# Modulation rows of a two-layer hybrid block moved and paired, last down tiles split once, values projected token-major

## The chip, the cores and the metric

The kernel runs on one core of a Trainium2 chip. The metric is the device time of one execution in microseconds (us); the number that stands for a kernel is the median of its runs. The engines that matter are TensorE (PE in the profile; its weight loads are PEld), VectorE (DVE), ScalarE (ACT), GpSimd (POOL) and SyncE (SP), which issues nearly all transfers.

## What is computed

A generator block of two layers over 512 latent tokens and 256 context tokens, 1024 channels. Cut to what matters here:

```python
for l in range(DEPTH):                       # 2 layers
    need_ctx = l < DEPTH - 1                 # context tokens only matter in layer 0
    sh1, sc1, g1, sh2, sc2, g2 = jnp.split(sc @ w_ada[l] + b_ada[l], 6, axis=-1)   # modulation
    ...
    h = rmsnorm(x, norm1_g[l]) * (1.0 + sc1) + sh1
    ...
    y, yc = hybrid_mixer(h, hc, w_in[l], ...)
    x = x + g1 * y
    h = rmsnorm(x, norm2_g[l]) * (1.0 + sc2) + sh2
    x = x + g2 * swiglu(h, w_ffn_gate[l], w_ffn_up[l], w_ffn_down[l])
    ...
# hybrid_mixer
aq, ak, av, bq, bzf, bzb, bi, bg, cu, cv, gt = split_proj(h @ w_in)
a = window_attention(...); b = hgrn_readout(hgrn2_bidir(... v=bi ...), bg, ...); c = chunk_mlp(cu, cv, ...)
# merge
g = sigmoid(gt.reshape(..., 3, D))
m = g[0] * (a @ w_br[0]) + g[1] * (b @ w_br[1]) + g[2] * (c @ w_br[2])
y = m @ w_o
```

In layer 0 all of it is done for the 512 latent and the 256 context tokens, 768 columns; in layer 1 the context matters only for keys, values and the HGRN states. `bi` are the values of the HGRN recurrence (4 heads of 128), `cv` the half of the gMLP that is mixed over tokens (4 tiles of 128 channels).

## The kernel before, in words

Activations lie channel-major: 128 channels on the partitions, tokens along the free axis. A projection (`dense`) takes one tile of 128 output channels: the weight tile (k x 128 x 128, k = 8 for 1024 inputs) is loaded raw by SP into one of three buffers (`wr`), ScalarE rounds it to its high half (`wh`), VectorE subtracts to get the low half (`wl`, line 296), and PE runs three matmuls per k (high by high, high by low, low by high) into a PSUM tile of 1024 columns (`pd`, two buffers). 768 tokens are a 512- and a 256-column matmul. The high and low halves of a weight tile have a buffer pair of their own kind, and the framework that orders the instructions puts the split of a tile about one tile ahead of its matmuls on each engine.

Work that PE needs little of runs as "chains", generators that `spent` steps on by an amount of PE time credited by `dense` (HGRN scans, norms, attention). SBUF beside the weights is cut in pages; a page is held as two halves (`single`) or whole (`pair`).

**Modulation.** A unit is 512 of the 6144 outputs of `w_ada`, 8 rows of 128 x 512. Layer 0's first four units are made at the start by matmul. The others go row by row on VectorE: `ada_accum` multiplies a row by the conditioning and adds it to `acc` (line 531; two `acc` where the context needs it too, one otherwise); after 8 rows a transpose and a reduce (lines 506, 507). `fill` takes one row from a queue through one buffer (`aw`), and asks for the next row's load once the row is used. `fill_unit` takes a whole unit, two rows per load, through `wr`. Before, 24 rows run as `fill_unit` between HGRN heads of layer 0, 48 in layer 0's merges (two `fill` for each of 24 tiles), others in layer 0's FFN, and 32 in layer 1's merges (two for each tile of the second and third branch).

**Order of a layer**: projections of the 4 HGRN heads; keys; attention with gMLP and HGRN gates between; merges (three branches, eight tiles `m` each: a gate tile of `w_in` with k = 8, a branch tile with k = 4, line 1300 on); output; FFN in pieces (gate and up tiles, then 8 down tiles for each piece). In layer 0's last FFN pieces the gate and up tiles are made by a scheme with seven products in place of eight (`seven`). The last piece's down tiles run once for each of two blocks of tokens (layer 0: 512 and 256, layer 1: 256 and 256), so that the norm that follows can begin on the first block; each block loads and splits its tiles anew. `norm_begin`, `start_settle` and `norm_end` make the next layer's input (`nt`, `hl`, lines 721 and 731).

**HGRN values and gMLP v.** Both are needed with tokens on the partitions. Before, they are projected channel-major, copied by ScalarE to `vf` or `cvs`, transposed on PE by 128 x 128 against an identity, and copied back (`V`, `cvt`).

## Time and profile before

| | us |
|---|---|
| median of 3 runs | 2484.31 (2484.30 to 2485.63) |
| profiled execution | 2482.72 |
| its span on the core | 2480.9 |
| projections of layer 0 | 47.5 to 533 |
| merges of layer 0 | 533 to 843 |
| output of layer 0 | 843 to 921.4 |
| FFN of layer 0, with its last down tiles | 921.4 to 1466 |
| projections of layer 1 | 1466 to 1836 |
| merges of layer 1 | 1836 to 2054 |
| output of layer 1 | 2054 to 2104 |
| FFN of layer 1, then the final norm | 2104 to 2480.9 |

The page is one execution taken by the hardware profiler. Names are those of the program: `pd<-hh,wl` is a matmul into a projection's PSUM tile from an activation and a weight half, and a line number is that of the kernel before. "Idle before" is the time that an engine stood still just before an instruction, with what ended it.

### The profile page before, as it was taken

The page shows a single profiled execution, that of the slowest core. Times are in us where ns is not written, and L with a number is a line of the kernel's source. Part 1 is how long each engine was busy: PE and PEld are TensorE (multiplying, and loading weights), DVE is VectorE, ACT ScalarE, POOL GpSimd, SP SyncE. Part 2 cuts the span into 40 slices and gives each one's busy share as a digit, 9 for nine tenths or more (in the row PEclk, how much of TensorE's full clock was granted, in tenths as well). Part 3 has the DMA queues.
Part 4 walks back from the last instruction along what each step waited for, and adds up shares of the span by engine and source line. Part 5 has one row for each costly group of instructions (what it writes and reads, how often), then busy time and mean ns, then how long its engine had stood idle before and what let it go on. Part 6 is the DMA issues. An engine that isn't in the chain of part 4 may idle for free. (4 is left out here: it accounts for less than half of the span.)

```text
span 2480.9 us, 34528 instructions
## 1 busy us (share of the span) xinstructions
PE 2397.0 (97%) x13606; PEld 2083.7 (84%) x13606; DVE 1555.1 (63%) x2644; ACT 900.3 (36%) x1508; POOL 308.9 (12%) x215
## 2 busy tenths in 40 slices
...
GB/s 295 70 77 81 48 43 35 39 64 112 142 133 73 78 118 43 115 111 110 95 127 111 107 144 52 43 43 52 60 44 152 124 151 168 79 106 100 91 103 130
DMA packets 370673, 240.02 MB, mean 97 GB/s; under 512 B 9744, under 2 KB 341968, under 8 KB 370512
## 3 DMA queue, kind: packets, MB, share of 16 engines
...
q8 instruction: 107, 1.75, 0.3%
...
q14 instruction: 54, 0.44, 0.1%
...
## 5 line engine op out<-in xcount | busy, mean ns | idle before, releaser
L295 ACT ACTIVATE wh<-wr 128x1024 fp32r<-128x1024 f32 (+4 forms) x344 | 308.0, 895 | 853.1 <-PE pd L313 727.2
L313 PE MATMUL pd<-hh,wl 128*128 128x512 f32 (+1 forms) x1504 | 451.9, 356 | 21.5 <-DVE wl L296 21.4
L296 DVE TENSOR_TENSOR wl<-wr,wh 128x1024 fp32r<-128x1024 f32 (+4 forms) x344 | 354.9, 1032 | 186.8 <-ACT wh L295 184.1
L313 PE MATMUL pd<-hh,wh 128*128 128x512 f32 (+1 forms) x1504 | 459.9, 362 | 0.7 <-ACT wh L295 0.6
L313 PE MATMUL pd<-hl,wh 128*128 128x512 f32 (+1 forms) x1504 | 446.7, 354 | 0.0
L313 PEld LDWEIGHTS pd<-hh,wl 128*128 128x128 f32 x1504 | 249.0, 190 | 65.7 <-DVE wl L296 28.9
L531 DVE SCALAR_TENSOR_TENSOR acc<-wra,sc,acc 128x512 f32<-128x512 f32 x224 | 169.6, 778 | 186.7 <-DMA wra<-in_w_ada 175.6
L313 PEld LDWEIGHTS pd<-hl,wh 128*128 128x128 f32 x1504 | 248.2, 190 | 34.4
L313 PEld LDWEIGHTS pd<-hh,wh 128*128 128x128 f32 x1504 | 249.7, 191 | 31.4 <-ACT wh L295 1.0
L313 PE MATMUL pd<-fh,wl 128*128 128x512 f32 (+1 forms) x496 | 175.3, 370 | 0.3 <-DVE wl L296 0.3
L313 PE MATMUL pd<-fl,wh 128*128 128x512 f32 (+1 forms) x496 | 175.7, 370 | 0.0
L313 PE MATMUL pd<-fh,wh 128*128 128x512 f32 (+1 forms) x496 | 174.4, 369 | 0.6 <-ACT silu L1370 0.6
L313 PE MATMUL pd<-guh,wh 128*128 128x512 f32 (+1 forms) x576 | 172.6, 341 | 1.8 <-ACT guh L760 0.9
L313 PE MATMUL pd<-guh,wl 128*128 128x512 f32 (+1 forms) x576 | 172.5, 340 | 1.8 <-DVE wl L296 1.8
L313 PE MATMUL pd<-gul,wh 128*128 128x512 f32 (+1 forms) x576 | 172.9, 340 | 0.1
L808 DVE SCALAR_TENSOR_TENSOR X<-pd,mod,X 128x256 f32<-128x256 f32 (+1 forms) x160 | 84.1, 560 | 85.3 <-PE pd L313 84.9
L313 PEld LDWEIGHTS pd<-guh,wh 128*128 128x128 f32 x576 | 98.3, 188 | 15.4 <-ACT guh L760 1.2
L313 PEld LDWEIGHTS pd<-guh,wl 128*128 128x128 f32 x576 | 98.6, 189 | 15.1 <-DVE wl L296 2.6
L313 PEld LDWEIGHTS pd<-gul,wh 128*128 128x128 f32 x576 | 98.7, 189 | 13.4 <-DVE gul L761 0.9
L313 PEld LDWEIGHTS pd<-fh,wl 128*128 128x128 f32 x496 | 90.1, 188 | 17.4 <-DVE wl L296 1.2
L313 PEld LDWEIGHTS pd<-fh,wh 128*128 128x128 f32 x496 | 89.5, 188 | 16.8 <-ACT silu L1370 0.8
L313 PEld LDWEIGHTS pd<-fl,wh 128*128 128x128 f32 x496 | 90.0, 188 | 15.5
...
## 6 DMA issues: line engine op xcount, KB each, us to landing
wr<-in_w_in SPq DMA_DIRECT2D x116, 512.0 KB, 3.9
wra<-in_w_ada SPq DMA_DIRECT2D x136, 256.0 KB, 2.8
wr<-in_w_ffn_gate SPq DMA_DIRECT2D x44, 512.0 KB, 3.9
wr<-in_w_ffn_up SPq DMA_DIRECT2D x44, 512.0 KB, 3.9
wr<-in_w_out SPq DMA_DIRECT2D x32, 512.0 KB, 3.7
wr<-in_w_branch SPq DMA_DIRECT2D x48, 256.0 KB, 3.0
wr<-in_w_ffn_down SPq DMA_DIRECT2D x48, 256.0 KB, 2.8
...
```

What stands on the lines that cost most here:

```text
L295: nc.scalar.activation(out=h, in_=r, func=AF.Copy)
L296: nc.vector.tensor_tensor(out=o, in0=r, in1=h.bitcast(F32), op=ALU.subtract)
L313: nc.tensor.matmul(ps[:, b0:b1], lhsT=w[:, k, :], rhs=x[:, b0:b1], start=b not in first, stop=(k == kt - 1 and i == 2), skip_group_check=True)
L531: nc.vector.scalar_tensor_tensor(out=acc[:, 0:512], in0=w, scalar=sc, in1=acc[:, 0:512], op0=ALU.mult, op1=ALU.add)
L808: self.nc.vector.scalar_tensor_tensor(out=self.X[m][:, c0:c1], in0=ps[:, c0:c1], scalar=gcol(b, m), in1=self.X[m][:, c0:c1], op0=ALU.mult, ...
```

## The change

1. `dense_tokens`: HGRN values for two heads at a time (with the even head), and gMLP v for two tiles at a time. The activations are the stationary operand (128 tokens), a weight block of 128 x 256 moves, the result has tokens on the partitions and is copied straight to `V` or `cvt`. The weights come as two loads of four k each. 768 tokens are six chunks, four in one `pd` and two in the other. The transposes and the copies through `vf` and `cvs` go.
2. Modulation: `fill_pairs` takes two rows per load of 512 KB through `wr`. Layer 0's merges take one pair per tile in place of two single rows. Layer 1's merges take none; of their 32 rows, 16 (units 8 and 9) are queued behind layer 0's merges, with one more `fill` in each group of seven products, and 16 (units 10 and 11) run as two pairs behind each of the first four gate and up tiles of layer 1's FFN.
3. `keep_w`: in the last FFN piece the first block splits each down tile into a page pair (`wk`), and the second block uses it again.
4. At the head of each branch of the merges, chains are stepped on until six page pairs are free.

The loads that SP issues go from 582 to 534, and PE's matmuls grow by 300 (192 in the HGRN values, 192 in gMLP v, 4 for the modulation, less 88 transposes).

VectorE in layer 0's merges, second branch, before: `acc` with two rows (each twice, for latent and context), `gt` the gate's product with the branch, `wl` of 512 columns a branch tile's split and of 1024 a gate tile's.

```order
L1323 SCALAR_TENSOR_TENSOR gt_6130<-gt_6130,pd_6138 128x768
L296 TENSOR_TENSOR wl_6233<-wr_6230,wh_6232 128x512
L531 SCALAR_TENSOR_TENSOR acc_6426<-wra_6665,sc,acc_6426 128x512
L531 SCALAR_TENSOR_TENSOR acc_6427<-wra_6665,sc,acc_6427 128x512
L531 SCALAR_TENSOR_TENSOR acc_6426<-wra_6724,sc,acc_6426 128x512
L531 SCALAR_TENSOR_TENSOR acc_6427<-wra_6724,sc,acc_6427 128x512
L506 STREAM_TRANSPOSE tr_6763<-acc_6426 128x512
L506 STREAM_TRANSPOSE tr_6766<-acc_6427 128x512
L507 TENSOR_REDUCE parts_5615<-tr_6763 128x16
L507 TENSOR_REDUCE parts_5615<-tr_6766 128x16
L296 TENSOR_TENSOR wl_6270<-wr_6267,wh_6269 128x1024
L1323 SCALAR_TENSOR_TENSOR gt_6228<-gt_6228,pd_6236 128x768
```

The same place now (the number in `wra_` is the load):

```order
L303 TENSOR_TENSOR wl_6562<-wr_6559,wh_6561 128x1024
L1357 SCALAR_TENSOR_TENSOR gt_6516<-gt_6516,pd_6524 128x768
L303 TENSOR_TENSOR wl_6619<-wr_6616,wh_6618 128x512
L565 SCALAR_TENSOR_TENSOR acc_6553<-wra_6745,sc,acc_6553 128x512
L565 SCALAR_TENSOR_TENSOR acc_6554<-wra_6745,sc,acc_6554 128x512
L565 SCALAR_TENSOR_TENSOR acc_6553<-wra_6745,sc,acc_6553 128x512
L565 SCALAR_TENSOR_TENSOR acc_6554<-wra_6745,sc,acc_6554 128x512
L303 TENSOR_TENSOR wl_6658<-wr_6655,wh_6657 128x1024
L1357 SCALAR_TENSOR_TENSOR gt_6614<-gt_6614,pd_6622 128x768
L303 TENSOR_TENSOR wl_6715<-wr_6712,wh_6714 128x512
```

Before, the rows of two loads stand between the two splits; now the four `acc` between them come from one load, with the same count of instructions per tile.

VectorE at layer 0's last down tiles, second block, before: `X` 128x256 is the residual of a down tile of that block, `wl` 128x512 a down tile's split, `nt` and `hl` the norm for layer 1.

```order
L808 SCALAR_TENSOR_TENSOR X_6771<-pd_12829,mod_141,X_6771 128x256
L680 TENSOR_TENSOR sqa_12800<-sqa_12800,sq_12820 128x512
L296 TENSOR_TENSOR wl_12875<-wr_12872,wh_12874 128x512
L649 TENSOR_SCALAR ms_12858<-st_12853 128x4
L808 SCALAR_TENSOR_TENSOR X_6771<-pd_12849,mod_141,X_6771 128x256
L296 TENSOR_TENSOR wl_12900<-wr_12897,wh_12899 128x512
L721 SCALAR_TENSOR_TENSOR nt_12916<-X_6771,A_12611,rsb_12885 128x512
L808 SCALAR_TENSOR_TENSOR X_6772<-pd_12878,mod_141,X_6772 128x256
L296 TENSOR_TENSOR wl_12927<-wr_12924,wh_12926 128x512
L731 SCALAR_TENSOR_TENSOR hl_12915<-nt_12916,mod_142,hh_12914 128x512
L808 SCALAR_TENSOR_TENSOR X_6772<-pd_12903,mod_141,X_6772 128x256
L721 SCALAR_TENSOR_TENSOR nt_12941<-X_6771,A_12611,rsb_12885 128x512
```

And now, from the last splits of kept tiles (`wk`) on:

```order
L797 TENSOR_TENSOR wk_12905<-wr_12906,wk_12905 128x512
L797 TENSOR_TENSOR wk_12867<-wr_12868,wk_12867 128x512
L844 SCALAR_TENSOR_TENSOR X_6853<-pd_12757,mod_141,X_6853 128x512
L844 SCALAR_TENSOR_TENSOR X_6853<-pd_12779,mod_141,X_6853 128x512
L303 TENSOR_TENSOR wl_13151<-wr_13148,wh_13150 128x1024
L303 TENSOR_TENSOR wl_13157<-wr_13154,wh_13156 128x1024
L844 SCALAR_TENSOR_TENSOR X_6854<-pd_12801,mod_141,X_6854 128x512
L844 SCALAR_TENSOR_TENSOR X_6854<-pd_12823,mod_141,X_6854 128x512
```

The splits between the residuals are gone, and the two splits of 1024 columns (layer 1's first two tiles) stand before the residuals of the first block. Behind these rows come those of the second block, with nothing between but the norm:

```order
L844 SCALAR_TENSOR_TENSOR X_6853<-pd_12961,mod_141,X_6853 128x256
L757 SCALAR_TENSOR_TENSOR nt_13016<-X_6853,A_12751,rsb_12991 128x512
L844 SCALAR_TENSOR_TENSOR X_6854<-pd_12984,mod_141,X_6854 128x256
L757 SCALAR_TENSOR_TENSOR nt_13035<-X_6853,A_12751,rsb_12991 128x512
L767 SCALAR_TENSOR_TENSOR hl_13015<-nt_13016,mod_142,hh_13014 128x512
L844 SCALAR_TENSOR_TENSOR X_6854<-pd_13003,mod_141,X_6854 128x256
L757 SCALAR_TENSOR_TENSOR nt_13060<-X_6854,A_12751,rsb_12991 128x512
L844 SCALAR_TENSOR_TENSOR X_6855<-pd_13024,mod_141,X_6855 128x256
```

SP at layer 1's first FFN tiles, before:

```order
L283 DMA wr_18763<-in_w_ffn_gate 128x8x128
L283 DMA wr_18769<-in_w_ffn_up 128x8x128
L283 DMA wr_18930<-in_w_ffn_gate 128x8x128
L283 DMA wr_18963<-in_w_ffn_up 128x8x128
L283 DMA wr_18997<-in_w_ffn_gate 128x8x128
L283 DMA wr_19030<-in_w_ffn_up 128x8x128
```

and now, with pairs of rows (`wra`) behind each up tile's load:

```order
L283 DMA wr_18835<-in_w_ffn_gate 128x8x128
L283 DMA wr_18841<-in_w_ffn_up 128x8x128
L665 DMA wra_19002<-in_w_ada 128x2x512
L665 DMA wra_19008<-in_w_ada 128x2x512
L283 DMA wr_19012<-in_w_ffn_gate 128x8x128
L283 DMA wr_19045<-in_w_ffn_up 128x8x128
L665 DMA wra_19079<-in_w_ada 128x2x512
L665 DMA wra_19083<-in_w_ada 128x2x512
L283 DMA wr_19090<-in_w_ffn_gate 128x8x128
L283 DMA wr_19123<-in_w_ffn_up 128x8x128
```

All go through the three `wr` buffers, so each load waits until the buffer of the third load before it is free.

The diff:

```diff
@@ -289,2 +289,9 @@
 
+    def keep_w(self, wap, kt):
+
+        pg = self.pair("wk", F32R)
+        hi, lo = pg[:, 0, 0:kt * P], pg[:, 1, 0:kt * P]
+        self.split(self.load_raw(wap, kt).rearrange("p k c -> p (k c)"), hi, lo)
+        return pg, tuple(t.rearrange("p (k c) -> p k c", c=P) for t in (hi, lo))
+
     def load_w(self, wap, kt):
@@ -324,2 +331,28 @@
 
+    def dense_tokens(self, wap, act, n, take):
+
+        nc = self.nc
+        half = KD // 2
+        ps = [self.pd.tile([P, 1024], F32, tag="pd", name=self.nm("pt")) for _ in range((n + 3) // 4)]
+        for h in (0, 1):
+            raw = self.wr.tile([P, KD, P], F32, tag="wr", name=self.nm("wr"))
+            hi = self.wh.tile([P, KD, P], F32R, tag="wh", name=self.nm("wh"))
+            lo = self.wl.tile([P, KD, P], F32R, tag="wl", name=self.nm("wl"))
+            r, wh, wl = (t.rearrange("p k c -> p (k c)") for t in (raw, hi, lo))
+            nc.sync.dma_start(out=r.rearrange("p (k c) -> p k c", c=2 * P),
+                              in_=wap[h * half * P:(h + 1) * half * P, :].rearrange("(k p) c -> p k c", p=P))
+            nc.scalar.activation(out=wh, in_=r, func=AF.Copy)
+            nc.vector.tensor_tensor(out=wl, in0=r, in1=wh.bitcast(F32), op=ALU.subtract)
+            for c in range(n):
+                for k in range(half):
+                    ah, al = (x[:, c * P:(c + 1) * P] for x in act[h * half + k])
+                    for i, (x, w) in enumerate(((ah, wh), (al, wh), (ah, wl))):
+                        nc.tensor.matmul(ps[c // 4][:, (c % 4) * 256:(c % 4 + 1) * 256], lhsT=x,
+                                         rhs=w[:, k * 256:(k + 1) * 256],
+                                         start=(h == 0 and c % 2 == 0 and k == 0 and i == 0),
+                                         stop=(h == 1 and k == half - 1 and i == 2), skip_group_check=True)
+                    self.spent(3 * (256 / 2400 + 0.0133))
+                if h and (c % 4 == 3 or c == n - 1):
+                    take(c // 4 * 4, ps[c // 4][:, 0:(c % 4 + 1) * 256].rearrange("p (c x) -> p c x", x=256))
+
     def spent(self, us):
@@ -444,2 +477,3 @@
         take(0, 0, be, u1)
+        self.fill()
         g2 = self.high_low(s21)
@@ -623,6 +657,8 @@
 
-    def fill_unit(self):
+    def fill_pairs(self, n=1):
 
-        assert self.ada_raw is None
-        for _ in range(KD // 2):
+        for _ in range(n):
+            if not self.ada_queue:
+                return
+            assert self.ada_raw is None
             raw = self.wr.tile([P, 2, 512], F32, tag="wr", name=self.nm("wra"))
@@ -833,8 +869,13 @@
                                         scalar2=None, op0=ALU.mult)
-        pv = self.dense(wcol(OFF_BI + hd * P), act, FULL)
-        vf = self.single("vf")
-        nc.scalar.copy(out=vf[:, 0:T], in_=pv[:, 0:T])
-        self.chains.append(self.hgrn_chain(l, hd, q, F, K, Q, vf, o_out, tq, qch, qbanks))
+        if hd % 2 == 0:
+            self.V = [self.single("V") for _ in (0, 1)]
+
+            def take(c, x):
+                for j, eng in ((0, nc.scalar.copy), (1, nc.vector.tensor_copy)):
+                    eng(out=self.V[j][:, c * P:(c + x.shape[1]) * P].rearrange("p (c f) -> p c f", f=P),
+                        in_=x[:, :, j * P:(j + 1) * P])
+            self.dense_tokens(self.a["w_in"][l][:, OFF_BI + hd * P:OFF_BI + (hd + 2) * P], act, NCH, take)
+        self.chains.append(self.hgrn_chain(l, hd, q, F, K, Q, self.V[hd % 2], o_out, tq, qch, qbanks))
 
-    def hgrn_chain(self, l, hd, q, F, K, Q, vf, o_out, tq, qch, qbanks):
+    def hgrn_chain(self, l, hd, q, F, K, Q, V, o_out, tq, qch, qbanks):
         nc = self.nc
@@ -849,5 +890,2 @@
         yield HEAD_US
-        V = self.single("V")
-        self.transpose_tokens(vf, V, NCH)
-        self.free(vf)
         for b, c0, c1 in qbanks:
@@ -1188,13 +1226,9 @@
                 yield None
-            ps = self.dense(wcol(OFF_CV + i * P), act, [(0, tt)])
-            f = self.single("cvs")
-            nc.scalar.copy(out=f[:, 0:tt], in_=ps[:, 0:tt])
-            for j in range(len(cvf)):
-                m = min(3, n - 3 * j)
-                bk = self.bank("cvp")
-                for c in range(m):
-                    nc.tensor.transpose(bk[:, c * P:(c + 1) * P], f[:, (3 * j + c) * P:(3 * j + c + 1) * P], self.ident)
-                nc.vector.tensor_copy(out=cap(cvf[j], i * P, [[512, m], [1, P]]),
-                                      in_=bk[:, 0:m * P].rearrange("p (c f) -> p c f", f=P))
-            self.free(f)
+            if i % 2 == 0:
+                def take(c, x, i=i):
+                    for d in range(c, c + x.shape[1]):
+                        eng = nc.scalar.copy if d % 2 else nc.vector.tensor_copy
+                        o = (d % 3) * 512 + i * P
+                        eng(out=cvf[d // 3][:, o:o + 2 * P], in_=x[:, d - c, :])
+                self.dense_tokens(self.a["w_in"][l][:, OFF_CV + i * P:OFF_CV + (i + 2) * P], act, n, take)
         mv = self.small("mv", 2 * NCH).rearrange("p (c x) -> p c x", x=2)
@@ -1276,3 +1310,3 @@
             if l == 0 and hd > 0:
-                self.fill_unit()
+                self.fill_pairs(4)
         self.attn_keys(act, wcol)
@@ -1301,3 +1335,3 @@
         if l == 1:
-            self.ada_units(1, (8, 9, 10, 11), 1)
+            self.ada_units(1, (10, 11), 1)
         for bi, (idx, src) in enumerate(((2, cc), (0, at), (1, o))):
@@ -1307,2 +1341,4 @@
                 self.finish_chains()
+            while self.chains and sum(h == [True, True] for h in self.pages.halves) < 6:
+                self.step_chain()
             br, brheld = self.split_pairs(src, tt, "br")
@@ -1310,4 +1346,2 @@
                 pg = self.dense(wcol(OFF_GT + idx * D + m * P), act, [(0, tt)])
-                if l == 0 or bi > 0:
-                    self.fill()
                 gt = self.single("gt")
@@ -1327,4 +1361,4 @@
                 self.free(gt)
-                if l == 0 or bi > 0:
-                    self.fill()
+                if l == 0:
+                    self.fill_pairs()
             self.free(*brheld)
@@ -1334,4 +1368,3 @@
             self.ada_units(1, (4, 5, 6, 7), 1)
-        else:
-            assert not self.ada_queue
+            self.ada_units(1, (8, 9), 1)
         self.dump(f"m{l}", macc[0][:, 0, :])
@@ -1378,3 +1411,5 @@
                 gu.append((hp[:, i % 2, :], lp[:, i % 2, :]))
-                if l == 0 and i > 0:
+                if l == 1:
+                    self.fill_pairs(2)
+                elif i > 0:
                     next(making)
@@ -1393,8 +1428,16 @@
             after = self.norm_shared if l == 0 else self.final_part
+            kept = []
             for bi, blk in enumerate(blocks if last else [(None, 0, tt)]):
                 for m in range(KD):
-                    ps = self.dense(a["w_ffn_down"][l][f0 * P:(f0 + n) * P, m * P:(m + 1) * P], gu, [blk[1:]])
+                    wap = a["w_ffn_down"][l][f0 * P:(f0 + n) * P, m * P:(m + 1) * P]
+                    if last:
+                        if bi == 0:
+                            kept.append(self.keep_w(wap, n))
+                        self.early.append(kept[m][1])
+                    ps = self.dense(wap, gu, [blk[1:]])
+                    if last and bi == 1:
+                        self.free(kept[m][0])
                     for bb in ([blk] if last else blocks):
                         self.add_res(m, ps, lambda b, m: self.mod[l][:, 40 + m, b:b + 1], bb)
-                    if n > 2:
+                    if l == 0 and n > 2:
                         self.fill()
@@ -1402,2 +1445,3 @@
                     self.drain()
+                assert l == 0 or not self.ada_queue
                 self.finish_chains()
```

## Prediction, made before the changed kernel ran

> **What bounds the kernel now.** I read the engines' totals first, then the span cut into its stages, then who waits for whom in the stages that the change touches, and last single instructions there. The first row of the page, then the windows by stage (length, PE busy and its instructions, granted clock, DMA share, GB/s):
>
> ```profile
> PE 2397.0 (97%) x13606; PEld 2083.7 (84%) x13606; DVE 1555.1 (63%) x2644; ACT 900.3 (36%) x1508; POOL 308.9 (12%) x215
> ...
> 533.00:843.00 310.00, 299.21 (x1696) 0.99 0.37 110
> ...
> 1424.00:1466.00 42.00, 39.35 (x228) 1.00 0.58 171
> ...
> 1836.00:2054.00 218.00, 210.58 (x961) 0.99 0.45 132
> ...
> 2162.00:2434.00 272.00, 272.00 (x1201) 1.00 0.34 98
> 2434.00:2471.50 37.50, 37.50 (x311) 1.00 0.44 129
> ```
>
> TensorE sets the time: it idles 2480.9 - 2397.0 = 84 us in all. So a change pays in three ways only: fewer or shorter matmuls, an idle stretch of PE that closes, and a stretch at half clock that no longer happens. The merges (533 to 843 in layer 0, 1836 to 2054 in layer 1) hold 10.8 and 7.4 us of idle. Layer 1's FFN (2162 to 2471.5) holds none; an edit there can only lose. The waits of PE in the two merge stages and around layer 0's last down tiles, in that order (total us, times, longest):
>
> ```profile
> PE pd L313 <- DVE wl L296: 10.8, 8, 3.1
> ...
> PE pd L313 <- DVE wl L296: 7.3, 6, 3.0
> ...
> PE pd L313 <- DVE wl L296: 5.1, 4, 3.3
> PE pd L313 <- ACT wh L295: 0.8, 2, 0.6
> ```
>
> All idle of PE in the merges ends with one thing, VectorE's split of a weight tile (wl). The timeline of VectorE shows why the split is late:
>
> ```profile
> 666.72 1.53 DVE L531 SCALAR_TENSOR_TENSOR acc<-wra,sc,acc 128x512 f32<-128x512 f32 x2 [1.38 <-DMA wra<-in_w_ada]
> 671.17 1.42 DVE L531 SCALAR_TENSOR_TENSOR acc<-wra,sc,acc 128x512 f32<-128x512 f32 x2 [2.92 <-DMA wra<-in_w_ada]
> ...
> 674.88 1.22 DVE L296 TENSOR_TENSOR wl<-wr,wh 128x1024 fp32r<-128x1024 f32 x1
> ```
>
> A modulation row (acc) waits 2.92 us for its load with the split queued behind it. The page's group of these rows says that this is the rule (busy, mean ns, idle before them and what ended it):
>
> ```profile
> L531 DVE SCALAR_TENSOR_TENSOR acc<-wra,sc,acc 128x512 f32<-128x512 f32 x224 | 169.6, 778 | 186.7 <-DMA wra<-in_w_ada 175.6
> ```
>  The row's buffer is single, so the next load starts only when the row before is used. And after a PE gap of this kind the granted clock is half for 3.4 us (two windows in layer 0's merges, one each at layer 1's start, in its merges, and behind the first transposes of the HGRN values; 3.4 us at 0.50 do 1.7 us of work, so each costs 1.7):
>
> ```profile
> 676.20:679.60 3.40, 3.40 (x11) 0.50 0.49 154
> 706.90:710.30 3.40, 3.40 (x13) 0.50 0.34 99
> ...
> 1471.50:1474.90 3.40, 3.40 (x12) 0.50 0.54 159
> 1925.50:1928.90 3.40, 3.18 (x8) 0.50 0.59 178
> 95.90:99.30 3.40, 3.40 (x17) 0.50 0.48 154
> ```
>
> **The change part by part.** The sum is made against the profiled run, 2482.72 us.
>
> *Matmuls.* Start-to-start times on PE: transposes, the 512+256 pair, 256 columns alone, 512 alone (a piece of the chain, 216 in 49.25 us):
>
> ```profile
> 94.92 0.88 PE L961 MATMUL tp<-ident,vf 128*128 128x128 f32 x6 [2.14 <-ACT vf L836]
> 95.63 1.65 PE L856 MATMUL hd<-q,Y 128*128 128x128 f32 x8
> ...
> 1000.11 0.51 PE L313 MATMUL pd<-guh,wl 128*128 128x512 f32 x2
> ...
> 1005.41 0.51 PE L313 MATMUL pd<-guh,wl 128*128 128x512 f32 x2
> ...
> 2059.82 0.28 PE L313 MATMUL pd<-mh,wl 128*128 128x256 f32 x1
> 2059.94 0.28 PE L313 MATMUL pd<-mh,wh 128*128 128x256 f32 x1
> ...
> 1945.56 49.25 PE pd L313 x216
> ```
>
> Six transposes take 95.63 - 94.92 = 0.71, so 0.118 each; a pair takes 5.30/15 = 0.353; 256 columns 0.12; 512 columns 0.228. A token-major projection of 768 tokens costs nine 256-column matmuls for each k and tile where there were three pairs: 9 x 0.12 - 3 x 0.353 = +0.02 to +0.03, over 12 tiles x 8 k = 96 places +2.4 at 0.1205. gMLP in layer 1 (512 tokens) has six for three: 6 x 0.1205 - 3 x 0.228 = +0.04, x 32 = +1.3. The 48 + 40 transposes go: -88 x 0.118 = -10.4. Sum **-6.7**, bounds -4 (had the transposes been partly in idle time) and -8.
>
> The Trainium skill, page "TensorE: Matmul & The Clock Gate", section "Back-to-back issue gap", gives N/2.4 + 2.5 ns between matmuls: 109 ns for 256 columns, 216 for 512. By that the 256-column form would cost about 1 us in all, not 3.7. The rows here lie above both figures (120 and 228), so the rows decide.
>
> *Waits around the values.* Who waits for the copies vf and cvs that go (us, times), and what evacuates them:
>
> ```profile
> L836 ACT COPY vf<-pd x8: 774/780/785, 94.1 to 1652.7; 128x768 f32<-128x768 f32 x8
> ...
>   PE tp L961: 6.6, 5
> ...
>   PE cvp L1196: 0.3, 1
> ```
>
> 6.6 + 0.3 go with the transposes, and the half-clock stretch at 95.9, 1.7: -8.6. In return the new call needs both projection accumulators for 768 tokens, so its matmuls for the last 256 tokens may wait until the evacuation before it is done, and the projection behind it waits for its copies. An evacuation takes 0.78; over six such calls that is between 0 and 2 x 0.78 x 6 = 9 us. I take 1: the copies are pieces of that row, dealt to ScalarE and VectorE, and the last tokens' matmuls come 4 x 12 x 0.12 = 5.8 us after the first. **-7.6**, from -8.6 to 0.
>
> *Layer 0's merges.* The same 48 rows, now two per load through the ring of three weight buffers. In the order, VectorE meets the four acc of a step behind a pair that was issued a step earlier, and a step is 8 + 4 k of PE pairs: 12 x 3 x 0.353 = 12.7 us. A landing (issues of the page, us last):
>
> ```profile
> wra<-in_w_ada SPq DMA_DIRECT2D x136, 256.0 KB, 2.8
> wr<-in_w_ffn_gate SPq DMA_DIRECT2D x44, 512.0 KB, 3.9
> ```
>
> takes 3.9 for 512 KB, a third of a step. VectorE's work in a step is four acc at 0.78, splits of 1.22 and 0.88 (the latter in a row further down) and the gate's product, at most 1.2 again: 6.4, half of it. So the 10.8 of idle and the two half-clock stretches (3.4) should go; I leave 2.5 for the places where attention chains and branch splits crowd VectorE (bounds 0 and 8). **-11.7**.
>
> *Layer 1's merges.* No rows any more: 7.3 and 1.7 go, 0.5 stays (0 to 4.5). **-8.5**. VectorE's acc there leave other work untouched, since PE waited for nothing else.
>
> *Layer 0's last down tiles and layer 1's start.* Two windows over the second block of tiles and the first projection of layer 1 (length, PE, PEld, DVE, ACT, POOL), and VectorE's groups from 1447.3 to 1475:
>
> ```profile
> 1447.30:1465.60 18.30, 15.65 (x118) 14.21 (x118) 15.77 (x25) 13.06 (x24) 8.94 (x9) 1.00 0.65 184
> 1465.60:1475.00 9.40, 5.51 (x19) 4.00 (x18) 9.16 (x15) 4.45 (x8) 3.27 (x2) 0.82 0.38 111
> ...
> L296 DVE TENSOR_TENSOR wl<-wr,wh 128x512 fp32r<-128x512 f32 x7 | 6.2, 881 | 1.1 <-ACT wh L295 1.1
> L721 DVE SCALAR_TENSOR_TENSOR nt<-X,A,rsb 128x512 f32<-128x512 f32 x8 | 5.8, 738 | 0.7 <-PE rsb L666 0.7
> ...
> L296 DVE TENSOR_TENSOR wl<-wr,wh 128x1024 fp32r<-128x1024 f32 x2 | 3.5, 1748 | 0.0
> ```
>
> Here VectorE is the bound: 24.9 of 27.7 us busy, while PE needs only 8 x 12 x 0.12 = 11.6 for the tiles. Kept tiles take 6.2 out of this stretch, and the first two splits of layer 1 (3.5) now stand before it. So up to 9.7; what is late next is the normalization itself (nt and hl behind each other on VectorE) and the POOL step between. I take 5.3 of it and the 1.7 of the clock at 1471.5: **-7** (-3 to -9.5). The splits of the first block cost what they did. In layer 1 the same edit gives 0: PE was full there (37.50 of 37.50).
>
> *What the moved rows cost.* 16 rows go into layer 0's FFN, one more in each group of seven. The waits there, and the rows already in it (busy, mean ns, idle before them):
>
> ```profile
> PE pa L413 <- DVE wl L761: 5.1, 4, 2.1
> ...
> L531 DVE SCALAR_TENSOR_TENSOR acc<-wra,sc,acc 128x512 f32<-128x512 f32 x70 | 53.5, 784 | 40.5 <-DMA wra<-in_w_ada 40.5
> ```
>
> Rows wait 40.5 us for loads, and 5.1 of PE's idle ends with a split on the same engine. 16 more in denser groups: in proportion 16/70 x 5.1 = 1.2; I take **+2** (-2, as others move, to +6). The last 16 go as pairs between the first four gate and up tiles of layer 1, again through the ring: four loads of 512 KB in a PE period of 2 x 24 x 0.228 = 10.9 us. Three buffers, each held for a landing of 3.9 and then 2 x 1.22 (ScalarE's half of the split taken as long as VectorE's) or 3.1 of acc, give 4 x 6.7/3 = 8.9: it fits narrowly, and by the order the splits of the third and fourth tile come about 1 us late. **+2** (0 to +6).
>
> **Sum**: -6.7 - 7.6 - 11.7 - 8.5 - 7 + 2 + 2 = -37.5, so 2445.2 for a run like the profiled one. The median of the shown runs is 1.6 above that (2484.31), so **2447**.
>
> **The rivals.**
>
> *The rows only move.* VectorE waits 175.6 us on loads of rows in the whole run, and PE's share of that in the merges is 18. If the denser rows in layer 0's FFN and the full ring in layer 1's find PE as tender as the merges did, 32 rows at the old price of (10.8 + 3.4 + 7.3 + 1.7)/80 = 0.29 us cost 9, and one or two half-clock stretches and a late first tile 5 more, where I had 4: 2447 + 10 = 2457, to 2462. For it: the fit in layer 1's FFN is narrow. Against: VectorE has the slack there, since PE was full.
>
> *Token-major calls stall.* Each of six calls waits twice for an evacuation, the gain of 7.6 is lost, and two half-clock stretches follow: 2447 + 8 + 4 = 2459. For it: 2.14 us in the first row of the matmuls is such a wait. Against: that one waits for a copy of all 768 tokens, and the new copies of the first 512 run while the last are still multiplied.
>
> *The idle in the merges was not the rows'.* Then the change doesn't do what it says: without rows the split would wait for something else, and 20 us come back: 2467. Against: no wait of PE in layer 0's merges ends with ScalarE.
>
> *Weight loads come to the front.* Every matmul has its own load (13606 of each in the first row), and at 2083.7/13606 = 0.153 us a load is longer than the 0.12 between 256-column matmuls. If that set their pace, the 1056 matmuls of the new form would lose 0.033 each, 35 us: 2482, no change. Against: the three rows of layer 1's output above are 0.12 apart with a load each. The Trainium skill, same page, section "LDWEIGHTS (loading the stationary operand)", has such a load at columns/1.2 ns, 107 ns for 128 columns, as long as the matmul it serves; the rows show it hidden.
>
> *Slower: the ring of three becomes the loop.* If two 512-KB loads issued together land in 7.8 instead of 3.9, a step of layer 0's merges is 3.1 (acc) + 7.8 + 2.4 + 0.9 = 14.2 instead of 12.7, and four loads in layer 1's FFN 4 x 10.6/3 = 14.1 instead of 10.9. That loses 24 x 1.5 + 4 x 3.2 = 49, and 10 of the merges' gain is not had: 2447 + 59 = 2506. It decides from a landing of 12.7 - 6.4 = 6.3 us on. Against it: the row below shows 216 GB/s, at which two such loads (1.05 MB) land in 4.9.
>
> ```profile
> 2471.50:2480.90 9.40, 2.34 (x20) 0.87 0.55 216
> ```
>
> **How the numbers follow.** Forecast 0.63; rows only move 0.15; calls stall 0.10; idle not the rows' 0.04; weight loads 0.02; ring is the loop 0.06. The best ends of the bounds give -8 - 8.6 - 14.2 - 9 - 9.5 - 2 + 0 = -51, so 2433; three rivals lie between 2457 and 2467; the worst ends of all terms at once (-4 + 0 - 6 - 4.5 - 3 + 6 + 6 = -5.5) are at 2479. The range is 2434 to 2474, which leaves out the last two rivals and the tails. A measurement of this kernel tells about 0.2% (5 us) from no change, so below 2479 is faster: 0.92 from the first four cases, less 0.05 for bad ends that meet, 0.87; slower 0.07, the ring and a little of those; 0.06 between.
>
> **What would show each step.** In the profile after: PE's waits on wl in both merge stages near 0 to 3 us, and no window at 0.50 there; no tp on vf and no cvp rows, and 256-column matmuls 0.12 apart (if 0.13 or more, the first term is wrong); the first projection of layer 1 over some 7 us sooner after the last down tile of the first block, with VectorE still its releaser; from the first gate tile of layer 1 to 2162's counterpart a loss of 0 to 6 us. It would be wrong if PE's idle in layer 0's FFN grew past 6 us, or if the splits in the merges waited for loads of weights (releaser DMA wr).

## The result, and the profile after

The changed kernel takes 2467.93 us (median of 3 runs, 2466.05 to 2468.98) where the kernel before took 2484.31: a ratio of 0.9936, with a 95% interval of 0.9917 to 0.9956. It is 16.4 us faster, where 37 were predicted. The time lies inside the predicted range; the gain is less than half of the predicted one.

The first row of the page after, and the windows by stage (length, PE busy, granted clock, DMA share, GB/s). The bounds are the first matmul of each stage (for the merges the first of a branch tile): projections of layer 0, merges, FFN with last down tiles, projections of layer 1, merges, then layer 1's first gate and up tiles and its last down tiles:

```profile
PE 2391.0 (97%) x13910; PEld 2097.4 (85%) x13910; DVE 1541.2 (62%) x2630; ACT 877.2 (36%) x1478; POOL 307.6 (12%) x215
...
48.61:531.95 483.34, 465.57 (x3172) 0.99 0.19 54
531.95:836.35 304.40, 304.39 (x1745) 1.00 0.39 113
909.29:1465.07 555.78, 533.88 (x2996) 0.99 0.37 111
1465.07:1826.47 361.40, 351.52 (x2292) 1.00 0.17 50
1826.47:2033.35 206.88, 206.68 (x968) 1.00 0.34 101
2083.52:2144.60 61.08, 58.03 (x304) 1.00 0.52 153
2416.60:2457.50 40.90, 38.55 (x308) 0.96 0.04 12
```

Both merge stages are full now, 304.39 of 304.40 and 206.68 of 206.88. The idle sits elsewhere: 21.9 us in layer 0's FFN, where it was 15.4 (544.29 us, 528.89 of them busy), and 5.4 in layer 1's FFN, which held 1.2 before. Measured with the same bounds (first matmul to first matmul of the next stage), the two traces compare so:

| stage | before | after | difference |
|---|---|---|---|
| projections of layer 0 | 483.8 | 483.3 | -0.4 |
| merges of layer 0 | 315.6 | 304.4 | -11.2 |
| output of layer 0 | 74.5 | 72.9 | -1.5 |
| FFN of layer 0, last down tiles | 544.2 | 555.8 | +11.6 |
| projections of layer 1 | 370.5 | 361.4 | -9.1 |
| merges of layer 1 | 218.8 | 206.9 | -11.9 |
| output of layer 1 | 49.1 | 50.2 | +1.0 |
| FFN of layer 1, last down tiles | 367.3 | 374.0 | +6.8 |

The sum with the start is -13.7, the difference of the two profiled spans (2480.9 and 2467.2). The merges and layer 1's projections gained 32 us. Layer 0's projections gained nothing, where some 10 of the predicted 14.3 belonged (an estimate: 48 of the 88 transposes, 64 of the 96 places, waits of 4.8 and the stretch at 95.9), and the two FFNs gave 18 back.

**Where layer 0's FFN lost.** The last down tiles became 4.3 us shorter, so the rest of the stage grew by 15.9. The third piece carries most of that, 9.3: its groups of seven products took 62.4 us and take 71.7. The fifth and the sixth grew by 4.0 and 3.2 (14 acc in each, before 10 and 11), and the fourth, with 12 acc where it had 19, shrank by 1.2. The third piece's window before and after (length, PE, PEld, DVE, ACT, POOL, clock, DMA share), then VectorE's rows in it, before and after, and PE's waits there after:

```profile
1079.04:1141.40 62.36, 60.82 (x339) 59.61 (x338) 36.18 (x46) 26.31 (x40) 22.94 (x16) 0.97 0.29 83
...
1067.47:1139.16 71.69, 62.20 (x339) 59.41 (x337) 48.84 (x64) 26.42 (x42) 24.30 (x16) 0.98 0.36 107
...
L531 DVE SCALAR_TENSOR_TENSOR acc<-wra,sc,acc 128x512 f32<-128x512 f32 x2 | 1.4, 749 | 0.0
...
L565 DVE SCALAR_TENSOR_TENSOR acc<-wra,sc,acc 128x512 f32<-128x512 f32 x16 | 14.0, 884 | 14.2 <-DMA wra<-in_w_ada 14.2
...
PE pa L446 <- DVE wl L797: 3.5, 3, 1.7
PE pa L446 <- DVE silu L505: 3.3, 2, 2.4
PE pa L446 <- DVE ptmp L505: 1.5, 1, 1.5
```

Before, this piece had 2 acc; now it has 16, which wait 14.2 us for their loads and make VectorE busy 12.7 us longer. PE waits for what stands behind them: splits (wl), and combinations of products (silu, ptmp).

**Where layer 1's FFN lost.** 3.0 us in the first tiles (61.1, before 58.1), and 3.8 at the last down tiles. In the first tiles no wait of PE ends with a split; the two longest end with the norm's sum of squares (sqa, 1.2 us) and with an activation of the first tile (silu, 1.1). At the last down tiles, the timelines of ScalarE and VectorE, and PE's wait:

```profile
2414.54 0.58 ACT L1403 ACTIVATE silu<-pd 128x512 f32<-128x512 f32 x1
2415.40 0.85 ACT L796 ACTIVATE wk<-wr 128x768 fp32r<-128x768 f32 x1 [0.28 <-DMA wr<-in_w_ffn_down]
2417.48 0.85 ACT L796 ACTIVATE wk<-wr 128x768 fp32r<-128x768 f32 x1 [1.23 <-DMA wr<-in_w_ffn_down]
2419.28 0.84 ACT L796 ACTIVATE wk<-wr 128x768 fp32r<-128x768 f32 x1 [0.95 <-DMA wr<-in_w_ffn_down]
2420.03 0.61 ACT L796 ACTIVATE guh<-silu 128x512 fp32r<-128x512 f32 x1
...
2418.36 0.96 DVE L797 TENSOR_TENSOR wk<-wr,wk 128x768 fp32r<-128x768 f32 x1 [1.11 <-ACT wk L796]
2419.23 0.68 DVE L1405 TENSOR_TENSOR silu<-pd,silu 128x512 f32<-128x512 f32 x1
...
2420.69 0.50 PE L320 MATMUL pd<-guh,wk 128*128 128x256 f32 x2 [2.13 <-ACT guh L796]
```

The high half of the last activation (guh) stands on ScalarE behind three splits of kept tiles, each of which waits for its load, and the product it is made from (L1405) on VectorE behind their other half. PE stops for 2.13 us, and a half-clock stretch follows (the fourth row of the next but one block).

**Why layer 0's projections gained nothing.** The waits on the transposes are gone. Three of PE's waits there, after (one of 3.8 us on the load of the gMLP weights, 3.7 before, is left out), and the timeline of VectorE and PE around the longest:

```profile
PE hl L911 <- DVE Q L923: 4.1, 4, 2.9
...
PE rsb L702 <- POOL rs L688: 2.2, 1, 2.2
PE sc L1116 <- DVE qs L1056: 2.1, 1, 2.1
...
108.10 1.54 DVE L565 SCALAR_TENSOR_TENSOR acc<-wra,sc,acc 128x512 f32<-128x512 f32 x2 [2.49 <-DMA wra<-in_w_ada]
109.56 1.04 DVE L915 COPY_PREDICATED A<-lvm,hl 128x512 f32<-128x512 uint8 x2
110.50 1.62 DVE L923 TENSOR_TENSOR Q<-Q,F 128x768 f32<-128x768 f32 x1
...
112.26 2.90 PE L911 MATMUL hl<-Q,Y 128*128 128x128 f32 x12 [2.91 <-DVE Q L923]
```

A modulation row waits 2.49 us for its load with the HGRN chain's product Q queued behind it: the same pattern as in the merges, at a place where PE's wait on Q was 0.7 us at most before. The other two gaps, on rsb and qs, are not the rows' (experiment 6). Beside each of these three gaps lies a half-clock stretch, as beside the one in layer 1's FFN:

```profile
111.75:115.15 3.40, 2.89 (x13) 0.51 0.00 0
203.91:207.31 3.40, 3.40 (x19) 0.51 0.40 146
439.42:442.82 3.40, 3.40 (x16) 0.51 0.00 0
...
2423.02:2426.42 3.40, 3.40 (x19) 0.56 0.02 5
```

### The profile page after: what moved, and what is told of

It is laid out like the page before. It is cut to its first block, busy times and chain, and to the rows that moved or that the text cites. A ratio compares the mean times of both kernels' runs of the same rounds, so it can differ in the third digit from the quotient of the medians.

```text
span 2467.2 us, 34896 instructions
## 1 busy us (share of the span) xinstructions
PE 2391.0 (97%) x13910; PEld 2097.4 (85%) x13910; DVE 1541.2 (62%) x2630; ACT 877.2 (36%) x1478; POOL 307.6 (12%) x215
## 4 chain that ended last, share of the span: by engine, by line
PE 62%; DVE 7%; DMA 5%; issue 4%; ACT 2%; POOL 2%; POOLq 0%; DVEq 0%; SPq 0%; ACTq 0%
PE pd L320 50%; DMA wra<-in_w_ada 4%; PE pa L446 3%; PE pt L350 2%; DVE acc L565 1%; PE hl L911 1%; PE pg L446 1%; DVE wl L303 1%; PE pb L446 1%; PE pT L1171 1%; PE sc L1116 1%; DMA wr<-in_w_ffn_down 1%; PE pv L1162 1%; DVE wl L797 1%; DVE gul L797 1%
## 5 line engine op out<-in xcount | busy, mean ns | idle before, releaser
L303 DVE TENSOR_TENSOR wl<-wr,wh 128x1024 fp32r<-128x1024 f32 (+4 forms) x296 | 304.9, 1030 | 203.2 <-ACT wh L302 200.9
L320 PE MATMUL pd<-hh,wh 128*128 128x512 f32 (+1 forms) x1280 | 392.5, 361 | 0.2 <-DVE q L857 0.2
L320 PE MATMUL pd<-hl,wh 128*128 128x512 f32 (+1 forms) x1280 | 385.6, 355 | 0.0
L320 PE MATMUL pd<-hh,wl 128*128 128x512 f32 (+1 forms) x1280 | 382.2, 353 | 0.0
L320 PE MATMUL pd<-gul,wh 128*128 128x512 f32 (+1 forms) x416 | 125.1, 357 | 0.6 <-DVE gul L797 0.3
L320 PE MATMUL pd<-guh,wh 128*128 128x512 f32 (+1 forms) x416 | 124.1, 355 | 1.4 <-ACT guh L796 0.9
L320 PE MATMUL pd<-guh,wl 128*128 128x512 f32 (+1 forms) x416 | 123.9, 354 | 0.0
L1360 POOL TENSOR_TENSOR macc<-macc,gt 128x768 f32<-128x768 f32 (+1 forms) x32 | 62.0, 1939 | 332.8 <-DVE gt L1357 332.8
L350 PE MATMUL pt<-wh,hh 128*128 128x256 f32 x352 | 102.8, 292 | 0.0
L716 POOL TENSOR_TENSOR sqa<-sqa,sq 128x256 f32<-128x256 f32 (+1 forms) x40 | 48.2, 1205 | 420.4 <-ACT sq L714 417.4
```

What stands on the lines that cost most here:

```text
L303: nc.vector.tensor_tensor(out=o, in0=r, in1=h.bitcast(F32), op=ALU.subtract)
L320: nc.tensor.matmul(ps[:, b0:b1], lhsT=w[:, k, :], rhs=x[:, b0:b1], start=b not in first, stop=(k == kt - 1 and i == 2), skip_group_check=True)
L350: nc.tensor.matmul(ps[c // 4][:, (c % 4) * 256:(c % 4 + 1) * 256], lhsT=x, rhs=w[:, k * 256:(k + 1) * 256], start=(h == 0 and c % 2 == 0 a ...
L716: eng.tensor_tensor(out=acc[:, c0:c1], in0=acc[:, c0:c1], in1=sq[:, c0:c1], op=ALU.add)
L1360: nc.gpsimd.tensor_tensor(out=mm, in0=mm, in1=gt[:, 0:tt], op=ALU.add)
```

## The experiments

Each time is a median beside runs of the kernel before on the same chip (2484 to 2485 us each time). Experiments 1 to 4, 5 to 8 and 9 to 12 ran on three different chips, and the kernel before differs by up to 1.1 us between them. Experiments 1 to 3 start from the changed kernel, 4 from the kernel before. Line numbers in the diffs' context are left out.

**1. Layer 1's tiles not kept.**

```diff
-                    if last:
+                    if last and l == 0:
                         if bi == 0:
                             kept.append(self.keep_w(wap, n))
...
-                    if last and bi == 1:
+                    if last and l == 0 and bi == 1:
                         self.free(kept[m][0])
```

> The changed kernel, but layer 1's last down tiles are loaded and split anew for the second block, as before the change; layer 0 keeps its tiles. In the changed kernel the stretch from the first last-down matmul of layer 1 to the last one grew from 37.2 to 40.9 us, with a 2.13-us wait on ScalarE's split of the last activation (guh), which stands behind six kept-tile splits that wait for their loads, and a half-clock stretch at 2422.6. Theory A (the kept splits on ScalarE hold the last activation back): that stretch returns to 37 us and the time falls by 3 to 4 us, to about 2464. Rival B (the gap comes from the shorter page or buffer supply, or from chance, and the kept tiles cost nothing): 2468, within 1 us of the changed kernel.

2464.24 us (ratio 0.9922, 0.9906 to 0.9938). The window of the last down tiles, and ScalarE there:

```profile
2413.49:2450.60 37.11, 37.11 (x308) 1.00 0.44 129
...
2413.46 0.85 ACT L302 ACTIVATE wh<-wr 128x768 fp32r<-128x768 f32 x1 [4.06 <-PE pd L320]
2414.49 0.63 ACT L796 ACTIVATE guh<-silu 128x512 fp32r<-128x512 f32 x1 [0.17 <-DVE silu L1405]
```

Theory A: the stretch is 37.1 again and PE is full. One split stands ahead of guh where there were three, and it was held by PE, which frees its buffer, and not by a load. This kernel is the base of most that follow.

**2. All 32 moved rows back in layer 1's merges, as pairs.**

```diff
         take(0, 0, be, u1)
-        self.fill()
...
-            self.ada_units(1, (10, 11), 1)
+            self.ada_units(1, (8, 9, 10, 11), 1)
...
-                if l == 0:
+                if l == 0 or bi > 0:
                     self.fill_pairs()
...
-            self.ada_units(1, (8, 9), 1)
...
-                if l == 1:
-                    self.fill_pairs(2)
-                elif i > 0:
+                if l == 0 and i > 0:
```

> The changed kernel, with the 32 moved rows back in layer 1's merges, but as pairs through the weight ring (one pair for each tile of the second and third branch); no extra row in the groups of seven products, none in layer 1's FFN. Theory A (the moved rows cost what they cost where they went: 9.3 us in the third FFN piece of layer 0, whose 16 acc wait 14.2 us for loads, and 3.0 in layer 1's first gate and up tiles; and pairs cost the merges nothing, as in layer 0): layer 0's FFN falls back by about 10 us, layer 1's first tiles by 3, layer 1's merges stay near 207 us: about 2455. Rival B (the waits of the FFN piece are those of another order of the same work, by the pages or the kept tiles): FFN of layer 0 stays within 3 us, total 2464 to 2468. Rival C (any row in layer 1's merges costs PE, paired or not): the merges grow back by 7 to 11 us, total 2462 to 2466.

2469.31 us (0.9944, 0.9926 to 0.9963). Layer 0's FFN fell to 543.5 us, 12.3 less than in the changed kernel, and layer 1's first tiles to 58.2: both as theory A said. But layer 1's merges rose from 206.9 to 222.9, more than before the change (218.8). The window and PE's wait there:

```profile
1811.89:2034.76 222.87, 213.41 (x976) 0.99 0.44 131
...
PE pd L320 <- DVE wl L303: 8.8, 9, 2.9
```

So theory A holds for the FFNs and rival C for the merges of layer 1, and worse than C had it; the total lies above what any of the three gave. VectorE's rows wait 49.0 us for their loads in this stage, where single rows waited 57.8 before the change, a pair often 4.5 to 5 us at a time. A step there takes PE 8.2 us by the spacing of the prediction (12 k x 3 x 0.228), not 12.7 as in layer 0. Pairs are not free by themselves. That the length of the step decides is argued from these two stages; no run varies it alone.

**3. Values and gMLP v as before the change.**

```diff
...
-            self.dense_tokens(self.a["w_in"][l][:, OFF_BI + hd * P:OFF_BI + (hd + 2) * P], act, NCH, take)
+        pv = self.dense(wcol(OFF_BI + hd * P), act, FULL)
+        vf = self.single("vf")
+        nc.scalar.copy(out=vf[:, 0:T], in_=pv[:, 0:T])
...
+        V = self.single("V")
+        self.transpose_tokens(vf, V, NCH)
+        self.free(vf)
...
+            ps = self.dense(wcol(OFF_CV + i * P), act, [(0, tt)])
+            f = self.single("cvs")
+            nc.scalar.copy(out=f[:, 0:tt], in_=ps[:, 0:tt])
...
```

> The changed kernel, with the HGRN values and gMLP v channel-major, copied and transposed as before the change. Layer 0's projections took 483.8 us before and 483.3 after, layer 1's 370.4 and 361.3. Theory A (the token-major form gained its matmuls, about 6.7 us, but in layer 0 its closed waits came back as waits of the chains on VectorE and GpSimd, 2.9 + 2.2 + 2.1 us, with two more half-clock stretches; so what it is worth is 3 us or less in layer 0 and about 3 in layer 1): the time rises by 3 to 7 us, to 2471 to 2475. Rival B (the token-major calls lose time of their own, and layer 1's gain is all from the kept tiles): same or faster than the changed kernel, 2464 to 2469. Rival C (the prediction's 14 us, hidden by something else that the change put into layer 0's projections): 2480 or more.

2469.61 us (0.9943, 0.9927 to 0.9958): 1.7 above the changed kernel, between what theory A and rival B gave. By stages, layer 1's projections rise by 6.8 (361.4 to 368.2), and layer 0's do not (483.3 to 482.9). So rival B is out, since the gain in layer 1 is mostly the values', and in layer 0 the form is worth nothing as the change stands. Of the total, 2.3 us go the other way in layer 1's last down tiles (40.9 to 38.6 by the traces), a place that the values do not touch, so the form is worth nearer an estimated 4 us than 1.7. The four runs' mean granted clock is 0.996, where the changed kernel's three have 0.994: over 2468 us an estimated 4 us more that the token-major kernel loses at half clock.

**4. The kernel before with layer 0's last down tiles kept, and nothing else.**

```diff
...
+                    if last and l == 0:
+                        if bi == 0:
+                            kept.append(self.keep_w(wap, n))
+                        self.early.append(kept[m][1])
+                    ps = self.dense(wap, gu, [blk[1:]])
...
```

> The kernel before, with layer 0's last down tiles split once and kept, and nothing else changed. In the changed kernel the stretch of these tiles is 4.3 us shorter and layer 1's projections 9.1 us, of which part is the token-major values. Theory A (the prediction's step of 7 us: VectorE freed of 6.2 us of splits, no half-clock stretch at layer 1's start): 2484.3 - 7 to 9 = 2475 to 2477. Rival B (the gain at layer 1's start belongs to the values): 2480 to 2482.

2475.68 us (0.9965, 0.9953 to 0.9978; its 7 runs lie between 2471.4 and 2484.5). Theory A: 9.5 us by the medians, 5.5 to 11.7 by the interval, where the prediction had 7. By the stages of the profiled run it is 6.6: the last down tiles take 37.8 us for 41.5, layer 1's projections 367.4 for 370.4.

**5. The 16 rows of the extra fills as pairs in layer 0's first FFN piece** (on experiment 1).

```diff
         take(0, 0, be, u1)
-        self.fill()
...
-                if l == 1:
+                if l == 1 or pi == 0:
                     self.fill_pairs(2)
-                elif i > 0:
+                if l == 0 and i > 0:
```

> The changed kernel without kept tiles in layer 1 (the first experiment, 2464), and with the 16 rows of the extra fills moved from the groups of seven products to layer 0's first FFN piece: two pairs behind each of its four gate and up tiles, as the change does in layer 1. A tile pair there takes PE 17 us (768 tokens) where layer 1's takes 10.9. Theory A (what the 16 rows cost, 12 us, they cost by waiting for single loads on VectorE in front of the splits of the groups of seven; as pairs beside tiles with slack they cost nothing): the first piece stays at 69.6 us, the rest of the FFN falls by 11 to 13, total about 2452. Rival B (rows cost about 0.7 us each wherever they stand): the first piece grows by 5 to 11, total 2458 to 2464.

2451.94 us (0.9872, 0.9855 to 0.9888), 12.3 below experiment 1. The first piece and the third, by windows:

```profile
910.36:979.91 69.55, 68.83 (x393) 59.34 (x391) 67.69 (x107) 27.36 (x43) 1.15 (x1) 1.00 0.38 112
1069.22:1129.98 60.76, 59.24 (x338) 58.04 (x337) 34.79 (x45) 25.87 (x40) 24.08 (x16) 1.00 0.32 92
```

Theory A: the first piece stays at 69.6 though VectorE is busy 67.7 of it, and the third is 10.8 shorter than experiment 1's 71.5. That the total fits to the microsecond is luck: by the traces layer 0's FFN is 15.9 shorter than in experiment 1, more than theory A had, and layer 0's projections, whose code is the same, are 5.9 longer. As many rows cost 12 to 16 us in one place and nothing in another. They also changed their form, from single rows to pairs; pairs within the groups of seven were not tried.

**6. The 24 rows of layer 0's HGRN stage moved into its attention stage** (on experiment 1).

```diff
-            if l == 0 and hd > 0:
-                self.fill_pairs(4)
...
                 done.append(units.pop(0)())
+                if l == 0:
+                    self.fill_pairs()
```

> The first experiment (2464), with the 24 rows that stand between the HGRN heads of layer 0 moved to the stage of attention, gates and gMLP behind them, one pair behind each of its twelve units. Theory A (in layer 0's HGRN stage the row in front of a chain's product, which waits 2.5 us for its load, makes PE's wait of 2.9 on Q and its half-clock stretch): that wait goes, the stage to 294 us is 3 to 5 us shorter; attention gives some of it back: 2460 to 2463. Rival B (Q would be late without rows: the transposes of the values used to give the chain its time): no change in that wait, 2464 to 2467.

2455.84 us (0.9885, 0.987 to 0.9899), 8.4 below experiment 1 and better than theory A had it. PE's waits there:

```profile
PE rsb L702 <- POOL rs L688: 2.2, 1, 2.2
PE sc L1116 <- DVE qs L1056: 1.9, 1, 1.9
...
PE hl L911 <- DVE Q L923: 1.0, 3, 0.4
```

The wait on Q was 4.1 in the changed kernel and 3.1 in experiment 1. The gaps on rsb and qs have stayed, so the rows are not their cause; with channel-major values (experiment 3) qs is 0.2 and rsb has none, so they came with the token-major form. Of the half-clock stretches of the projections one is left, the one after the load of the gMLP weights, which was there before. The projections take 471.4 us (482.5 in experiment 1). More of the attention's matmuls now fall into the merges (96 matmuls that are not projections, where there were 62), which take 308.8 for 300.6; both stages together are 2.9 shorter in the profiled runs. The mean granted clock of the four runs is 0.9965, of experiment 1's 0.9942: over 2460 us an estimated 5 to 6 of the 8.4 us. So by this estimate most of the gain is half-clock stretches that no longer happen. Why the two gaps that stayed draw none here isn't shown.

**7. The extra rows without their loads** (on experiment 1). The extra row in each group of seven uses the data of a row that is already there, so 18 loads are left out and the modulation has other values; VectorE's work stays.

```diff
         take(0, 0, be, u1)
-        self.fill()
+        if self.ada_queue and self.ada_raw is not None:
+            self.ada_step(self.ada_raw[:, 0, :])
...
+        self.ada_raw = None
```

> The first experiment (2464), where the extra row in each group of seven products is multiplied from the row that is in the buffer already: VectorE does the same work, but 18 loads of rows are left out (so the modulation has other values). Theory A (the 12 us in layer 0's FFN are waits for loads of single rows in front of splits): FFN of layer 0 falls by 8 to 12 us, total 2452 to 2456. Rival B (it is VectorE's added work, 16 rows x 0.78 and what they fold): FFN stays within 3 us of 555, total 2462 to 2465.

2459.97 us, 4.3 below experiment 1: between the two, nearer to rival B. The third piece, and its rows:

```profile
1063.63:1132.78 69.15, 62.08 (x338) 59.41 (x337) 49.96 (x65) 26.53 (x42) 24.88 (x16) 0.98 0.34 103
...
L566 DVE SCALAR_TENSOR_TENSOR acc<-wra,sc,acc 128x512 f32<-128x512 f32 x17 | 14.2, 847 | 5.8 <-DMA wra<-in_w_ada 5.8
```

The wait for loads fell from 14.2 to 5.8 us, and the piece from 71.5 (experiment 1) to only 69.2, where it takes 60.8 without the rows. So at least a third of the 12 us is waiting for loads; 5.8 us of such waits are still in this run. The rest is put down to them and to the rows' own work in front of splits and combinations that PE needs within a group of seven; how it divides isn't shown.

**8. gMLP v as before the change, HGRN values token-major** (on experiment 1; the last lines of experiment 3's diff).

> The first experiment (2464), with gMLP v channel-major and transposed as before the change; the HGRN values stay token-major. Undoing both cost 6.8 us in layer 1's projections and nothing in layer 0's. Theory A (the gain in layer 1 is the HGRN values', 24 transposes and the waits at vf; gMLP v, whose 16 transposes take 1.9 us and whose matmuls of 256 columns add 1.3, gives nothing): layer 1's projections within 1 us of 362, total 2463 to 2466. Rival B (gMLP v carries half of it): layer 1's projections 365 to 367, total 2466 to 2469.

2466.06 us (0.9911 to 0.9941), 1.8 above experiment 1; layer 1's projections 363.8 (363.0 in experiment 1). The total is on the border of the two. By the stage, 0.8 of the 6.8 us of experiment 3, theory A is the nearer: gMLP v is worth little, the HGRN values carry the gain.

**9. Both moves, experiments 5 and 6 together.**

> The first experiment (2464) with both moves of rows: the 24 of layer 0's HGRN stage into its attention stage (2456 alone), and the 16 of the extra fills into the first FFN piece (2452 alone). Theory A (they are independent): 2464 - 8 - 12 = 2443 to 2445. Rival B (the attention rows' gain was one of fewer half-clock stretches by chance): 2449 to 2452.

2446.44 us (0.9839, 0.9819 to 0.986). The sum of the two gains would be 2443.5, so 18 of 20.7 us add up, between theory A and rival B. The mean granted clock is 0.9955 where experiment 5 has 0.9928, an estimated 6 to 7 us over 2450, so what the second move adds (5.5 us) is again a matter of half-clock stretches. It is the fastest kernel here, 21 us below the changed one, with its edits but for the kept tiles of layer 1, and with rows in other places.

**10. The last 16 rows too in layer 0's first FFN piece** (on experiment 9).

```diff
-        if l == 1:
-            self.ada_units(1, (10, 11), 1)
...
-            self.ada_units(1, (8, 9), 1)
+            self.ada_units(1, (8, 9, 10, 11), 1)
...
-                if l == 1 or pi == 0:
-                    self.fill_pairs(2)
+                if l == 0 and pi == 0:
+                    self.fill_pairs(4)
```

> As the kernel with both moves, and the last 16 rows too go from layer 1's first gate and up tiles to layer 0's first FFN piece: four pairs behind each of its four tiles. Theory A (the room there holds: six loads in 17 us through three buffers, VectorE some 44 us of rows and 20 of other work in 69.6): layer 1's first tiles fall back from 61.1 to 58.1, the first piece stays at 69.6: 3 us below the kernel with both moves, 2440 to 2442. Rival B (VectorE or the ring is full): the first piece grows by more than 3 us, the total is 2444 or more.

2464.33 us (0.9915, 0.9893 to 0.9937). The first piece:

```profile
902.90:991.45 88.55, 74.95 (x401) 63.77 (x400) 81.89 (x131) 28.18 (x43) 1.14 (x1) 0.92 0.44 135
```

Rival B: 19 us longer, with VectorE busy 81.9 of 88.6. Of my 64 us of VectorE work the 20 that are not rows were too few: in experiment 1, without any row in this piece, it is busy 45.7 us there (it also makes the quarter sums for the groups of seven). PE waits 10.4 us on splits, 7.3 of them at once. What was free at 67.7 of 69.6 is the dearest place of all with 16 rows more.

**11. Experiment 6 with values and v as before the change.**

> The kernel with the rows of layer 0's HGRN stage in the attention stage (2456), but with the values and gMLP v channel-major and transposed as before the change. Theory A (in layer 0 the token-major form gained nothing only because rows stood in front of the chains' products; with the rows away it is worth there what it is in layer 1, 7 us or more): 2456 + 13 to 16 = 2469 to 2472. Rival B (in layer 0 the form is worth nothing by itself, and moving the rows gains with either form): 2456 + 5 to 8 = 2461 to 2464.

2469.62 us (0.9941, 0.9919 to 0.9963), 13.8 above experiment 6. Theory A. PE's wait on the transposes is larger than ever:

```profile
PE tp L997 <- ACT vf L872: 9.4, 4, 2.4
```

With experiment 3: the same edit is worth 1.7 us (nearer 4) with the rows between the heads and 13.8 without them. The projections and merges of layer 0 together take 786.7 us here and 780.2 in experiment 6, layer 1's projections 366.3 and 361.7. So 6.5 of the 13.8 lie in layer 0. But the wait on the transposes was 4.6 us in the kernel before and 4.9 in experiment 3: about half of the 9.4 came only when the rows moved.

**12. Single rows in layer 0's merges again** (on experiment 1).

```diff
+                if l == 0:
+                    self.fill()
                 gt = self.single("gt")
...
                 if l == 0:
-                    self.fill_pairs()
+                    self.fill()
             self.free(*brheld)
```

> The first experiment (2464), with the rows of layer 0's merges single again, two for each tile through the one buffer, as before the change; the same 48 rows. Theory A (the pairs are what closed the merges of layer 0, 11 to 15 us): the merges take 312 to 317 us, waits on the split (wl) of some 10 us and half-clock stretches are back: 2474 to 2479. Rival B (the merges got shorter because the chains come in another order since the values are token-major): the merges stay within 3 us of 301: 2463 to 2467.

2475.7 us (0.996, 0.9947 to 0.9974), 11.5 above experiment 1. In the profiled run, the fastest of its eight, the merges take 308.8 us (300.6 with pairs), and the wait that the change closed is back, though only in part and with no half-clock stretch:

```profile
PE pd L320 <- DVE wl L303: 3.5, 3, 2.6
```

Theory A by the time; by this one trace the pairs account for 8 of the 11 to 15 us, less than A's bounds for the stage. Rival B, the merges within 3 us, is out.

## Why the prediction went wrong

| term | predicted | measured | by |
|---|---|---|---|
| matmuls and waits of the values | -14.3 | -1.7 | experiment 3 (nearer -4); -13.8 with the rows moved, experiment 11 |
| layer 0's merges | -11.7 | -11.2 | stages; -11.5 by experiment 12 |
| layer 1's merges | -8.5 | -11.9 | stages |
| layer 0's last down tiles, layer 1's start | -7 | -9.5 | experiment 4; -6.6 by its stages |
| rows in layer 0's FFN | +2 | +12.3 | experiment 5; +15.9 by the stages |
| rows in layer 1's FFN | +2 | +3.0 | stages; 58.2 without them, experiment 2 |
| kept tiles in layer 1 | 0 | +3.8 | experiment 1 |
| sum | -37.5 | -15 | |

The right-hand sum is within 2 us of the measured -16.4. Its terms come partly from medians and partly from stages of single traces, each good to a few microseconds, so such a fit is partly luck; but no large term is left without a name.

**Right.** The reading of the merges: all idle of PE there ended with a split behind a row that waited, and now both stages are full, with no half-clock stretch. Layer 1's merges gained more than the 9.0 of idle and half clock that I counted. So did layer 0's last down tiles. Yet in layer 0 the waits of the rows themselves are not gone, as the prediction had it with a pair "issued a step earlier". VectorE's rows in that stage, and one step's:

```profile
L565 DVE SCALAR_TENSOR_TENSOR acc<-wra,sc,acc 128x512 f32<-128x512 f32 x84 | 60.1, 766 | 78.8 <-DMA wra<-in_w_ada 60.8 <-ACT acc L563 18.0
...
663.09 2.74 DVE L565 SCALAR_TENSOR_TENSOR acc<-wra,sc,acc 128x512 f32<-128x512 f32 x4 [3.88 <-DMA wra<-in_w_ada]
```

The rows wait 60.8 us for loads where they waited 77.3. A step has one such wait in place of two, and 3.9 us of it with 2.7 of acc fit into 12.7 without making a split late. The size of this term was right, and one part of its reason was not.

The cost of the 256-column form was read rightly. From the first start to the 28th, 27 intervals:

```profile
83.81 0.28 PE L350 MATMUL pt<-wh,hh 128*128 128x256 f32 x1
...
87.05 0.28 PE L350 MATMUL pt<-wh,hh 128*128 128x256 f32 x1
```

The starts stand 3.24/27 = 0.120 us apart, though each of these matmuls has a weight load of its own, so the rival in which weight loads come to the front is out. By the Trainium skill's formula for a single isolated matmul ("TensorE: Matmul & The Clock Gate", "Back-to-back issue gap") it would be 109 ns for 256 columns, 9% below that; the measurement decides.

**Wrong, first: "in proportion 16/70 x 5.1 = 1.2; I take +2".** This step of the sum failed by 10 us. It spread the rows evenly over a stage of 500 us and priced them by that stage's mean wait. The rows did not go there evenly: 14 more acc went into a piece that had 2, and whose chain of splits, products and combinations is short. I had counted by groups of seven how many rows come, and not in which piece, though the order of the program tells it. It also priced only PE's waits on splits. PE's waits in the stage before, then after:

```profile
PE pa L413 <- DVE wl L761: 5.1, 4, 2.1
PE pa L413 <- DVE silu L471: 3.3, 3, 2.2
...
PE pa L413 <- DVE ptmp L471: 0.9, 2, 0.5
...
PE pa L446 <- DVE silu L505: 6.9, 6, 2.4
PE pa L446 <- DVE wl L797: 6.1, 4, 2.6
PE pa L446 <- DVE ptmp L505: 4.2, 5, 1.5
```

The wait on splits grew by 1.0, close to the 1.2 of the proportion. The waits on the combinations (silu and ptmp), which stand in the same queue, grew by 6.9, and they were not in the sum. The prediction's own sign that this step is wrong, PE's idle in that stage growing past 6 us, came: 15.4 to 21.9, by 6.5. The rival "the rows only move" had the mechanism; its price, 0.29 us per row, was too low as well (experiment 5: 12.3/16 = 0.77). In layer 1's first tiles the +2 came out at +3.0 by another path: not at splits of the third and fourth tile, but at the norm and the first tile; and the 3.1 us of acc for a pair there was twice too much, since that modulation needs one acc for a row.

**Wrong, second: the return of 1 in "-7.6, from -8.6 to 0".** Experiment 11 gives 13.8 for the 14.3, but that is partly luck: the wait on the transposes that it closes is 9.4 us where the kernel before had 4.6 in that stage. What failed is the question what is late next. I looked for the new wait at the accumulators, and no wait on them is in the trace. It came on Q in the HGRN chains, which stands behind the rows that run between the heads (2.9 us), and on rsb and qs (2.2 and 2.1), and with these came half-clock stretches; why the token-major form brought the last two isn't shown. I saw those rows in layer 0's merges and FFN and did not ask after the 24 in the first stage, because the change does not touch them.

**Wrong, third: "In layer 1 the same edit gives 0".** PE was full there, I argued. A full PE says that an edit can't gain, not that it can't lose. The splits of kept tiles run ahead as loads and pages allow, past the one activation that PE needs first.

The measured 2468 lies beside the 2467 of the rival "the idle in the merges was not the rows'", but that is a coincidence: that idle is gone. The range held the time through its room for rivals and bad ends, not through the sum. The rival "token-major calls stall" had the half-clock stretches, at other waits than the evacuations that it named. The slower one (the ring of three as the loop) did not come in layer 0's merges. It did not come in layer 1's first tiles beyond the bound that I gave them, either.

What stays open: why layer 0's FFN and projections differ by some microseconds between profiled runs that share their code there, beyond the half-clock stretches; what a pair within a group of seven would cost; and why experiment 12's profiled merges lost less than the medians.
